# A feed-forward stage with one beside-step per product, low parts split row by row, and residual rows fetched one step sooner

## The chip, the cores and the metric

The kernel runs on one core of a Trainium2 chip. The metric is the time of one execution in device microseconds (us), and the number that counts is the median over runs. The engines are named as the profile names them: PE is TensorE (matmuls), PEld its weight loads, DVE is VectorE, ACT is ScalarE, POOL is GpSimd, SP is SyncE, which here only issues DMAs.

## What is computed

One layer of a streaming encoder, for 2048 prompt tokens and 32 tokens of a running stream, 2080 in all, with 1024 channels: a group of four mixers behind one input projection, and then a gated feed-forward block. The change touches only the second.

```python
x = x + jnp.einsum('ble,ed->bld', mix, w_out[l])
f = rms_norm(x, g_ffn[l])
hid = jax.nn.silu(jnp.einsum('bld,df->blf', f, w_gate[l])) * jnp.einsum('bld,df->blf', f, w_up[l])
x = x + jnp.einsum('blf,fd->bld', hid, w_down[l])
...
y = rms_norm(x, g_final)
```

The hidden width (D_FF) is 2816. All is float32.

## The kernel before

Precision: each float32 operand is split into a high part `hi` (rounded to the PE's fp32r type by an ACT copy) and a low part `lo = x - hi` (a subtraction on POOL or DVE). Each product is three matmuls: w_hi·x_hi, w_lo·x_hi, w_hi·x_lo.

The mixers fill the first 655 us. The feed-forward stage behind them is the other 1470 us. It goes over the tokens in three passes of two chunks each (346 or 348 tokens per chunk), and in each pass over 11 groups `g` of hidden columns. For a group it forms the gate block and then the up block. Each block is a 2x2 block product done with seven products instead of eight; their seven operands, sums and differences of normalized rows, are called p1, p5, p7, p6, p2, p3, p4 in the order of use (`ORDER`). One product is 12 matmuls of 128x128 weights by 346 columns (`wide`, lines 1134 to 1136). After each product about one or two finished pieces of the down projection run (`down`, lines 1149 to 1151), each of six matmuls into one of three PSUM banks, which DVE adds to the residual rows `xs` (line 1152). A "step" is one product with what belongs to it, so a group has 14 steps and a pass 154.

What stands beside the products, on engines whose order is written out by hand:

- **Evacuation of products.** DVE adds a product to a kept sum (lines 1205, 1207, 1227, 1235), multiplies gate and up (1237), ACT makes the high part of the hidden rows (1240) and DVE the low part (1241). In an up block the last four of the seven products have this work, the first three have none.
- **Weights.** DVE forms sums of weight quarters (1050, 1051, 1054, 1057), ACT rounds them (1019), POOL makes their low parts (1020).
- **Beside-work.** Generators in a list `ahead`, of which only the first is advanced in this stage (`active[0] = 1`). `sums_of` makes the next pass's seven operands: per channel row it loads four rows (line 902), waits two turns, then does seven DVE steps (906 to 941) and stores them to `td` in DRAM. `finish` normalizes the rows of the pass that has ended: seven steps of an ACT square and a DVE addition (1347, 1349), then eight DVE scalings (1403), each behind a load issued two rows ahead (1378). After each step of `finish` stands a `yield WAIT`.
- **fill(budget)** is called once per product, after its matmuls have been queued and before its evacuation. It advances the first generator until the budget is used up or the generator says WAIT. A step costs 0.55 to 0.6; the budget is 1.2 (or 0.8) in a gate block and 0.6 (or 0.6) in an up block, and what is overdrawn is owed (`debt`).
- **part(p, name)** turns a stored operand into hi and lo: a load of 128 x 1384 (958), an ACT copy (960) and the subtraction (963), which POOL does for the first two of four rows and DVE for the other two, one instruction each. This happens for 5 operands at the start of the stage, and for 7 in the last up block of the first and of the second pass (a "turn").
- **turn_over**: when the last pieces of a pass are added, its rows are written out (`away`, 1425) and the next pass's residual rows are loaded into the same tile four steps later (`residual`, 1446).

DVE, PE, ACT, POOL and SP each work through their instructions in the order written, so an instruction that waits holds up those behind it.

Of the kernel before, what the change touches and what calls it, by code (L numbers as in the profile page):

```python
# [7 lines left out]
F32 = mybir.dt.float32  # L8
# [26 lines left out]
FPASSES = ((0, 1), (2, 3), (4, 5))  # L35
NG = NFB // 2
H = KT // 2
# [48 lines left out]
def trunk_kernel(ctx: ExitStack, tc: tile.TileContext, a):  # L86
    nc = tc.nc
# [16 lines left out]
    def col(name, i):  # L104
# [5 lines left out]
        out=ident, in_=ident, compare_op=ALU.not_equal, fill=1.0, base=0,  # L110
# [144 lines left out]
    WAIT, LATE, DONE = object(), object(), object()  # L255

    debt = [0.0]

    def fill(budget):
        budget -= debt[0]  # L260
        late = []
        i = 0
        while budget > 0 and i < min(active[0], len(ahead)):
            step = next(ahead[i], DONE)
            if step is DONE:
                ahead.pop(i)
            elif step is WAIT or step is LATE:
                if step is LATE:
                    late.append(ahead[i])
                i += 1  # L270
            else:
                budget -= step
        while budget > 0 and spare:
            step = next(spare[0], DONE)
            if step is DONE:
                spare.pop(0)
            elif step is WAIT:
                break
            else:
                budget -= step  # L280
        for g in late:
            while (step := next(g, DONE)) is not WAIT:
                if step is DONE:
                    ahead.remove(g)
                    break
                budget -= step
        debt[0] = max(-budget, 0.0)
# [3 lines left out]
    def need(*names):  # L291

        for name in names:
            for _ in made[name]:
                pass

    def start(name, gen, spot=None):
        made[name] = gen
        ahead.insert(len(ahead) if spot is None else spot, gen)
# [79 lines left out]
    with ExitStack() as st:  # L379
# [402 lines left out]
        h = {}  # L782
# [164 lines left out]
    def place(p, name):  # L947
        pool, tag, bufs = {"p1": (wgt, "p1", 1), "p5": (wgt, "p5", 1)}.get(name, (bigp, "big", NCH))
        t = pool.tile([P, 2, H * FN], F32R, tag=tag, name="f_" + name, bufs=bufs)
        hi, lo = t[:, 0], t[:, 1]  # L950
        f[p][name] = rows_in(hi, p), rows_in(lo, p)
        return hi, lo

    def part(p, name):

        n = FCH[FPASSES[p][0]]
        hi, lo = place(p, name)
        nc.sync.dma_start(out=lo[:, : H * n].bitcast(F32), in_=td[p, name][:, : H * n])
        yield
        nc.scalar.copy(out=hi[:, : H * n], in_=lo[:, : H * n].bitcast(F32))  # L960
        yield
        for eng, o in ((nc.gpsimd, slice(0, H // 2 * n)), (nc.vector, slice(H // 2 * n, H * n))):
            eng.tensor_sub(out=lo[:, o], in0=lo[:, o].bitcast(F32), in1=hi[:, o].bitcast(F32))  # L963

    def first_operands():

# [174 lines left out]
    step = [0]  # L1141
# [24 lines left out]
    budget = [1.0]  # L1166
    events = []

    def at(k, fn):

        events.append((step[0] + k, fn))
        events.sort(key=lambda e: e[0])


    def block(p, evac, after=lambda k: None):
# [5 lines left out]
        def form(name, b, fresh=True, less=0.0):  # L1181
            if fresh:
                bank[b] = ps_mm.tile([P, 512], F32, tag="mm", name="pw")[:, :n]
            w = wq.take(step[0])
            wide(w, f[p][name], n, bank[b], fresh, True)
            fill(budget[0] - less * (budget[0] > 1))
# [183 lines left out]
    def finish(c):  # L1370

        n = FCH[c]
        got = {}

        def load(k):
            if k < KT:
                got[k] = row("xf")[:, :n]
                nc.sync.dma_start(out=got[k], in_=away[c, k // H][:, k % H * n : (k % H + 1) * n])

        def rows(k):  # L1380
            load(k + 2)
            return got.pop(k)

        load(0)
        load(1)
        yield WAIT
        gen = norm_scales(c, rows)
        while True:
            try:
                v = next(gen)  # L1390
            except StopIteration as e:
                r = e.value
                break
            yield v
            if v == 0.55:
                yield WAIT
        load(0)
        load(1)
        yield WAIT
        y = a["y"][P * KT * FO[c] : P * KT * (FO[c] + n)].rearrange("(p f) -> p f", p=P)  # L1400
        for k in range(KT):
            x = rows(k)
            nc.vector.scalar_tensor_tensor(
                out=x, in0=x, scalar=col("g_final", k), in1=r[:, :n], op0=ALU.mult, op1=ALU.mult
            )
            nc.sync.dma_start(out=y[:, k * n : (k + 1) * n], in_=x)
            yield 0.55
            yield WAIT
# [11 lines left out]
    def turn_over(p, h):  # L1420

        for i, c in enumerate(FPASSES[p]):
            n = FCH[c]
            away[c, h] = dramp.tile([P, H * FN], F32, tag="away_%d_%d" % (c, h), name="away", bufs=1)
            nc.sync.dma_start(out=away[c, h][:, : H * n], in_=halfs[c, h][:, : H * n])
            at(4, lambda i=i: residual(FPASSES[p + 1][i], h))
        if h:
            at(8, lambda: [start(("finish", c), finish(c)) for c in FPASSES[p]])

# [11 lines left out]
    def residual(c, h):  # L1441

        n = FCH[c]
        t = halfs[c, h] = late.tile([P, H * FN], F32, tag="xs", name="xs", bufs=4)
        v = t[:, : H * n].rearrange("p (k n) -> p k n", n=n)
        nc.sync.dma_start(out=v, in_=x2d[:, h * H : (h + 1) * H, FO[c] : FO[c] + n])
        for k in range(H):
            xs[c, h * H + k] = v[:, k]

    last = len(FPASSES) - 1  # L1450
    def put_part(p, name, first=1):

        gen = part(p, name)
        for k in (first, first + 2):
            at(k, lambda: next(gen))
        at(first + 3, lambda: [None for _ in gen])
# [14 lines left out]

    while ("squares", 3) not in made:
        next(made["fstats", 3])
    active[0] = 1
    for p in range(len(FPASSES)):
        for g in range(NG):
            if g == 2 and p < last:
                start(("sums", p + 1), sums_of(p + 1))
            before = after = lambda k: None
            if p == 0 and g == 0:  # L1480
                before = first_parts
            if p < last and g == NG - 1:
                need(("sums", p + 1))
                after = lambda k: put_part(p + 1, ORDER[k])
            gen = None
            if p < last or g < NG - 1:
                gen = quarters(g)
            hid = ffn_pair(p, g, before, after, gen)
            if gen:
                down_later(p, g, hid, gen)  # L1490
# [3 lines left out]
    n = FCH[cb]  # L1494
# [36 lines left out]
    def by_pool(c, k, rs):  # L1531
# [2 lines left out]
        nc.scalar.activation(out=g[:, :n], in_=x, func=AF.Copy, scale=col("g_final", k))  # L1534
        nc.gpsimd.tensor_mul(out=x, in0=g[:, :n], in1=rs[:, :n])

    while ahead:
        fill(100.0)
    for m in range(KT):
# [115 lines left out]
```

## Time and profile before

| what | value |
|---|---|
| median of 3 runs | 2127.08 us (2125.25 to 2128.69) |
| the profiled execution, its own time | 2125.5 us |
| its span | 2123.8 us |
| PE busy | 2027.5 us (95%) |
| DVE busy | 1444.6 us (68%) |
| POOL busy | 1138.5 us (54%) |
| ACT busy | 767.5 us (36%) |
| granted PE clock, mean | 0.982 |

The span is from the first to the last instruction of the program; 1.7 us of the execution's time lie around it. A busy time counts an engine's instructions, not its waits.

### The profile page before, as it was taken

The page shows a single profiled execution, that of the slowest core. Times are in us where ns is not written, and L with a number is a line of the kernel's source. Part 1 is how long each engine was busy: PE and PEld are TensorE (multiplying, and loading weights), DVE is VectorE, ACT ScalarE, POOL GpSimd, SP SyncE. Part 2 cuts the span into 40 slices and gives each one's busy share as a digit, 9 for nine tenths or more (in the row PEclk, how much of TensorE's full clock was granted, in tenths as well). Part 3 has the DMA queues.
Part 4 walks back from the last instruction along what each step waited for, and adds up shares of the span by engine and source line. Part 5 has one row for each costly group of instructions (what it writes and reads, how often), then busy time and mean ns, then how long its engine had stood idle before and what let it go on. Part 6 is the DMA issues. An engine that isn't in the chain of part 4 may idle for free.

```text
span 2123.8 us, 31916 instructions
## 1 busy us (share of the span) xinstructions
PE 2027.5 (95%) x11902; PEld 1980.8 (93%) x11902; DVE 1444.6 (68%) x2207; ACT 767.5 (36%) x1472; POOL 1138.5 (54%) x891
## 2 busy tenths in 40 slices
PE   8699998999997999999999999999999999999997
PEld 7689997899897999999998999999998999999997
DVE  3896599499576677556557676787557577656555
ACT  5423232332334333333334343333334333333332
POOL 2523352243335655656668565666667556655664
PEclk9899998999998999999999999999999999999998
DMA  7634233113367445222224534543224534422221
GB/s 214 177 94 112 71 116 112 41 61 124 108 168 206 137 136 153 85 71 78 78 99 146 188 97 128 159 151 124 75 86 148 195 103 136 133 70 75 75 80 59
DMA packets 152011, 247.88 MB, mean 117 GB/s; under 512 B 23440, under 2 KB 101008, under 8 KB 151216
## 3 DMA queue, kind: packets, MB, share of 16 engines
q1 hardware_dynamic: 149136, 245.67, 37.4%
q8 instruction: 94, 1.54, 0.3%
q14 instruction: 61, 0.50, 0.1%
q10 hardware_dynamic: 2720, 0.18, 0.1%
HBM read 209.42 MB, written 36.36 MB: 116 GB/s over the span
## 4 chain that ended last, share of the span: by engine, by line
PE 51%; DVE 18%; issue 11%; POOL 10%; DMA 7%; ACT 2%; SPq 1%; POOLq 0%; DVEq 0%; ACTq 0%
PE pw L1136 8%; PE pw L1134 8%; PE pw L1135 8%; DVE cv L726 6%; POOL wlo L1020 6%; PE pd L1150 5%; PE pd L1149 5%; PE pd L1151 5%; PE ps L230 4%; PE ps L232 4%; PE ps L231 3%; POOL dlo L1277 2%; DMA line<-rt 2%; DMA xk<-in_x 1%; POOL f_p L963 1%
## 5 line engine op out<-in xcount | busy, mean ns | idle before, releaser
L1136 PE MATMUL pw<-f_p,whi 128*128 128x346 f32 (+1 forms) x1848 | 598.4, 324 | 10.6 <-POOL f_p L963 10.5
L1134 PE MATMUL pw<-f_p,whi 128*128 128x346 f32 (+1 forms) x1848 | 597.5, 323 | 9.0 <-DVE sg L1227 6.0
L1135 PE MATMUL pw<-f_p,wlo 128*128 128x346 f32 (+1 forms) x1848 | 596.3, 323 | 0.0
L1020 POOL TENSOR_TENSOR wlo<-sum,whi 128x512 fp32r<-128x512 f32 x264 | 354.6, 1348 | 288.7 <-ACT whi L1019 285.7
L1152 DVE TENSOR_TENSOR xs<-pd,xs 128x346 f32<-128x346 f32 (+1 forms) x528 | 262.7, 512 | 240.3 <-PE pd L1151 240.2
L1136 PEld LDWEIGHTS pw<-f_p,whi 128*128 128x128 f32 x1848 | 350.1, 189 | 13.6 <-POOL f_p L963 13.6
L1134 PEld LDWEIGHTS pw<-f_p,whi 128*128 128x128 f32 x1848 | 351.5, 190 | 11.7 <-issue 8.3
L1135 PEld LDWEIGHTS pw<-f_p,wlo 128*128 128x128 f32 x1848 | 350.3, 190 | 0.3 <-POOL wlo L1020 0.3
L1277 POOL TENSOR_TENSOR dlo<-raw,dhi 128x256 fp32r<-128x256 f32 x256 | 223.0, 891 | 227.3 <-ACT dhi L1276 224.6
L1149 PE MATMUL pd<-hhi,dhi 128*128 128x346 f32 (+1 forms) x1024 | 330.4, 323 | 15.0 <-DVE xs L1152 15.0
L1150 PE MATMUL pd<-hhi,dlo 128*128 128x346 f32 (+1 forms) x1024 | 329.7, 322 | 0.1
L138 POOL TENSOR_TENSOR wlo<-raw,whi 128x1024 fp32r<-128x1024 f32 x67 | 183.9, 2749 | 269.9 <-ACT whi L137 268.1
L1151 PE MATMUL pd<-hlo,dhi 128*128 128x346 f32 (+1 forms) x1024 | 328.5, 321 | 0.0
L1020 POOL TENSOR_TENSOR wlo<-raw,whi 128x512 fp32r<-128x512 f32 x199 | 275.4, 1392 | 36.6 <-ACT whi L1019 36.4
L1019 ACT CAST whi<-sum 128x512 fp32r<-128x512 f32 x264 | 163.8, 621 | 295.7 <-DVE sum L1054 106.4
L230 PE MATMUL ps<-hi,whi 128*128 128x416 f32 x640 | 236.0, 369 | 8.5 <-ACT hi L214 4.1
L231 PE MATMUL ps<-hi,wlo 128*128 128x416 f32 x640 | 229.5, 359 | 6.6 <-POOL wlo L138 6.0
L232 PE MATMUL ps<-lo,whi 128*128 128x416 f32 x640 | 230.9, 361 | 3.2 <-POOL lo L207 3.0
L726 DVE SCALAR_TENSOR_TENSOR cv<-z,par,cv 128x416 f32<-128x416 f32 (+2 forms) x180 | 216.4, 1263 | 1.0 <-ACT cv L720 0.9
L1149 PEld LDWEIGHTS pd<-hhi,dhi 128*128 128x128 f32 x1024 | 192.8, 188 | 19.8 <-DVE xs L1152 19.2
L1150 PEld LDWEIGHTS pd<-hhi,dlo 128*128 128x128 f32 x1024 | 192.5, 188 | 1.9 <-POOL dlo L1277 1.5
L1151 PEld LDWEIGHTS pd<-hlo,dhi 128*128 128x128 f32 x1024 | 193.0, 189 | 0.0
(185 smaller groups left out, 2863.0 us busy)
## 6 DMA issues: line engine op xcount, KB each, us to landing
raw<-in_w_up SPq DMA_DIRECT2D x132, 256.0 KB
raw<-in_w_gate SPq DMA_DIRECT2D x128, 256.0 KB
raw<-in_w_down SPq DMA_DIRECT2D x256, 128.0 KB
raw<-in_w_in SPq DMA_DIRECT2D x43, 512.0 KB
raw<-in_w_out SPq DMA_DIRECT2D x24, 512.0 KB
f_p<-td SPq DMA_DIRECT2D x14, 692.0 KB
xt<-in_xt SPq DMA_DIRECT2D x20, 416.0 KB
x<-in_x SPq DMA_DIRECT2D x5, 1664.0 KB
```

What stands on the lines that cost most here:

```text
L230: nc.tensor.matmul(out, whi, xhi, start=start and k == 0, stop=False)
L231: nc.tensor.matmul(out, wlo, xhi, start=False, stop=False)
L232: nc.tensor.matmul(out, whi, xlo, start=False, stop=stop and k == n - 1)
L726: nc.vector.scalar_tensor_tensor(out=cv[:, t, :n], in0=z[:, t, j : j + n], scalar=col("w_conf", 31 * t + j), in1=cv[:, t, :n], op0=ALU.mul ...
L1020: nc.gpsimd.tensor_sub(out=lf, in0=src, in1=hf.bitcast(F32))
L1134: nc.tensor.matmul(ps, whi[:, k], xhi[:, k, :n], start=start and k == 0, stop=False, **more)
L1135: nc.tensor.matmul(ps, wlo[:, k], xhi[:, k, :n], start=False, stop=False, **more)
L1136: nc.tensor.matmul(ps, whi[:, k], xlo[:, k, :n], start=False, stop=stop and k == H - 1, **more)
L1149: nc.tensor.matmul(ps, whi, hhi[:, :n], start=i == 0, stop=False)
L1150: nc.tensor.matmul(ps, wlo, hhi[:, :n], start=False, stop=False)
L1151: nc.tensor.matmul(ps, whi, hlo[:, :n], start=False, stop=i == 1)
L1277: nc.gpsimd.tensor_sub(out=lf, in0=raw, in1=hf.bitcast(F32))
```

## The change

Three edits. From the start of the three passes on, `fill` ends after one step that did work, whatever the budget says (the flag `single`). The low parts of an operand are made by four instructions of one row each, the first on POOL and three on DVE. And the residual rows of the next pass are asked for three steps after the others were sent away, where it was four.

```diff
             else:
-                budget -= step
+                budget = 0 if single[0] else budget - step
...
-        for eng, o in ((nc.gpsimd, slice(0, H // 2 * n)), (nc.vector, slice(H // 2 * n, H * n))):
-            eng.tensor_sub(out=lo[:, o], in0=lo[:, o].bitcast(F32), in1=hi[:, o].bitcast(F32))
+        for k in range(H):
+            o = slice(k * n, (k + 1) * n)
+            (nc.vector if k else nc.gpsimd).tensor_sub(
+                out=lo[:, o], in0=lo[:, o].bitcast(F32), in1=hi[:, o].bitcast(F32)
+            )
...
-            at(4, lambda i=i: residual(FPASSES[p + 1][i], h))
+            at(3, lambda i=i: residual(FPASSES[p + 1][i], h))
...
     active[0] = 1
+    single[0] = True
...
+    single[0] = False
     while ahead:
         fill(100.0)
```

What it moves, in three places. The line numbers of the changed kernel are up to seven higher.

First, the instructions of DVE in the second pass's second up block, where `finish` squares a chunk's rows (`ssum<-ssum,sq` is its step). Before:

```order
L1349 TENSOR_TENSOR ssum<-ssum,sq 128x348
L1235 TENSOR_TENSOR u_11229<-pw,u_11335 128x346
L1237 TENSOR_TENSOR sg<-u_11229,sg 128x346
L1241 TENSOR_TENSOR hlo<-sg,hhi 128x346
L1152 TENSOR_TENSOR xs<-pd,xs 128x346
L1054 TENSOR_TENSOR sum<-sum,raw 128x512
L1349 TENSOR_TENSOR ssum<-ssum,sq 128x348
L1235 TENSOR_TENSOR u_11335<-pw,u_11335 128x346
L1237 TENSOR_TENSOR sg<-u_11335,sg 128x346
L1241 TENSOR_TENSOR hlo<-sg,hhi 128x346
L1152 TENSOR_TENSOR xs<-pd,xs 128x346
L1349 TENSOR_TENSOR ssum<-ssum,sq 128x348
```

The same products on DVE in the changed kernel:

```order
L1239 TENSOR_TENSOR u_11253<-pw,u_11359 128x346
L1241 TENSOR_TENSOR sg<-u_11253,sg 128x346
L1245 TENSOR_TENSOR hlo<-sg,hhi 128x346
L1156 TENSOR_TENSOR xs<-pd,xs 128x346
L1058 TENSOR_TENSOR sum<-sum,raw 128x512
L1353 TENSOR_TENSOR ssum<-ssum,sq 128x348
L1239 TENSOR_TENSOR u_11359<-pw,u_11359 128x346
L1241 TENSOR_TENSOR sg<-u_11359,sg 128x346
L1245 TENSOR_TENSOR hlo<-sg,hhi 128x346
L1156 TENSOR_TENSOR xs<-pd,xs 128x346 x2
L1061 TENSOR_TENSOR sum<-raw,sum 128x512
L1353 TENSOR_TENSOR ssum<-ssum,sq 128x348
```

A step of `finish` stood before every product's evacuation; now it stands before every second one, because the WAIT behind it takes a product of its own. `sums_of`, which did up to two or three steps in a product of a gate block, does one.

Second, DVE at the first turn, the low parts of two operands (`f_p`) among the last up block's evacuations. Before:

```order
L1237 TENSOR_TENSOR sg<-pw,sg 128x348
L1241 TENSOR_TENSOR hlo<-sg,hhi 128x348
L1152 TENSOR_TENSOR xs<-pd,xs 128x348
L963 TENSOR_TENSOR f_p_10272<-f_p_10272 128x692
L1235 TENSOR_TENSOR u_10212<-pw,u_10321 128x348
```

And in the changed kernel:

```order
L1241 TENSOR_TENSOR sg<-pw,sg 128x348
L1245 TENSOR_TENSOR hlo<-sg,hhi 128x348
L1156 TENSOR_TENSOR xs<-pd,xs 128x348
L965 TENSOR_TENSOR f_p_10282<-f_p_10282 128x346 x3
L1239 TENSOR_TENSOR u_10222<-pw,u_10331 128x348
```

One instruction of two rows became three of one row in the same place. On POOL each `f_p` row reads 128x346 where it read 128x692, also in the same place.

Third, SP after the first half of a pass's rows has been sent away. Before:

```order
L1425 DMA away<-xs 128x1392 x2
L1265 DMA raw<-in_w_down 128x256 x4
L1446 DMA xs<-x2d 128x4x346 x2
L1027 DMA raw<-in_w_up 128x512 x2
```

And in the changed kernel:

```order
L1429 DMA away<-xs 128x1392 x2
L1450 DMA xs<-x2d 128x4x346 x2
L1269 DMA raw<-in_w_down 128x256 x4
L1031 DMA raw<-in_w_up 128x512 x2
```

The residual rows now stand ahead of four loads of down weights. PE's own order is the same up to the place of four small matmuls per chunk of `finish`, and nothing changes ahead of the feed-forward stage.

## Rows read from the trace of the kernel before

**Rows 1.** The page's first line.
```profile
span 2123.8 us, 31916 instructions
```
**Rows 2.** Windows: us, busy PE PEld DVE ACT POOL (instructions), clock, DMA, GB/s.
```profile
655.00:700.00 45.00, 33.98 (x180) 31.78 (x178) 23.62 (x31) 15.43 (x25) 27.89 (x19) 0.81 0.76 211
...
1120.00:1160.00 40.00, 34.92 (x207) 32.49 (x206) 33.73 (x42) 19.15 (x33) 33.73 (x23) 1.00 0.38 130
```
**Rows 3.** Waits of PE, 655 to 700: who, for whom, total us, times, longest.
```profile
PE pw L1136 <- POOL f_p L963: 5.5, 2, 3.2
PE pw L1134 <- ACT f_p L960: 3.0, 1, 3.0
PE tok L147 <- DVE ssum L346: 2.5, 1, 2.5
```
**Rows 4.** Waits of PE, 700 to 1120.
```profile
PE pw L1134 <- DVE sg L1227: 3.4, 2, 3.1
```
**Rows 5.** Waits of PE, 1120 to 1160, the first turn.
```profile
PE pd L1149 <- DVE xs L1152: 2.5, 3, 1.2
PE pw L1136 <- POOL f_p L963: 2.5, 3, 1.4
```
**Rows 6.** Waits of PE, 1160 to 1600.
```profile
PE pd L1149 <- DVE xs L1152: 5.0, 3, 2.4
PE pw L1134 <- DVE sg L1227: 1.7, 3, 1.0
```
**Rows 7.** Waits of PE, 1640 to 2060, the row that differs from rows 6.
```profile
PE pw L1134 <- DVE sg L1227: 1.0, 2, 0.8
```
**Rows 8.** Waits of DVE, 700 to 2060, three of eleven rows.
```profile
DVE ssum L1349 <- ACT sq L1347: 20.9, 17, 3.8
DVE xf L906 <- DMA xf<-x2d: 11.6, 5, 4.1
...
DVE xf L1403 <- DMA xf<-away: 7.9, 4, 3.6
```
**Rows 9.** Timeline of DVE, 1218 to 1236: start, us, instruction, [idle before <- releaser].
```profile
1223.82 1.31 DVE L1349 TENSOR_TENSOR ssum<-ssum,sq 128x348 f32<-128x348 f32 x1 [1.14 <-ACT sq L1347]
...
1226.66 0.52 DVE L1241 TENSOR_TENSOR hlo<-sg,hhi 128x346 fp32r<-128x346 f32 x1 [0.55 <-ACT hhi L1240]
```
**Rows 10.** Timeline of PE, 1228 to 1236, its two waits.
```profile
1227.66 0.42 PE L1149 MATMUL pd<-hhi,dhi 128*128 128x346 f32 x1 [0.91 <-DVE xs L1152]
...
1233.41 0.43 PE L1149 MATMUL pd<-hhi,dhi 128*128 128x346 f32 x1 [1.68 <-DVE xs L1152]
```
**Rows 11.** Timeline of DVE, 1120 to 1158, the first turn.
```profile
1131.76 1.39 DVE L1241 TENSOR_TENSOR hlo<-sg,hhi 128x348 fp32r<-128x348 f32 x1 [0.55 <-ACT hhi L1240]
...
1133.50 0.86 DVE L963 TENSOR_TENSOR f_p<-f_p 128x692 fp32r<-128x692 f32 x1
...
1137.83 1.93 DVE L963 TENSOR_TENSOR f_p<-f_p 128x692 fp32r<-128x692 f32 x1
```
**Rows 12.** Timeline of POOL, the same stretch.
```profile
1130.79 1.98 POOL L963 TENSOR_TENSOR f_p<-f_p 128x692 fp32r<-128x692 f32 x1
1135.75 1.34 POOL L1020 TENSOR_TENSOR wlo<-sum,whi 128x512 fp32r<-128x512 f32 x1 [2.98 <-ACT whi L1019]
1137.06 1.95 POOL L963 TENSOR_TENSOR f_p<-f_p 128x692 fp32r<-128x692 f32 x1
```
**Rows 13.** Groups by form, DVE, 700 to 2060: busy us, mean ns, idle before.
```profile
L963 DVE TENSOR_TENSOR f_p<-f_p 128x692 fp32r<-128x692 f32 x14 | 20.8, 1488 | 0.0
```
**Rows 14.** Groups by form, POOL, 640 to 2060.
```profile
L963 POOL TENSOR_TENSOR f_p<-f_p 128x692 fp32r<-128x692 f32 x14 | 28.7, 2048 | 0.0
```
**Rows 15.** Timeline of SP's DMA issues, 1164 to 1176.
```profile
1164.26 1.49 SPq L1425 DMA_DIRECT2D away<-xs  x2
1165.80 5.94 SPq L1265 DMA_DIRECT2D raw<-in_w_down  x4
1171.84 2.06 SPq L1446 DMA_DIRECT2D xs<-x2d  x2
```

More of the change, by code (lines that the diff above doesn't have):

```diff
@@ L257, in trunk_kernel @@
     debt = [0.0]
+    single = [False]
     def fill(budget):
```

## The prediction

> **What bounds the kernel now.** I read the page first. Its span is 2123.8 us [rows 1]; the profiled execution took 2125.5, so 1.7 lie around the span, and the median of the three runs shown, 2127.1, is 1.6 above that execution. PE is busy 95% of the span, so the feed-forward stage is bound by PE's own matmuls, which the change leaves as they are. What a change of order can win there is the time in which PE stands still. So the second view was the list of PE's waits, cut into stretches so that each cause has its place.
>
> Between 700 and 2060 us four stretches are quiet or almost so, and their waits have one look: PE waits for DVE, either to free a PSUM bank (the piece of the down projection at line 1149 waits for the addition into `xs`) or to finish with a product (line 1134 waits for `sg`). That is 3.4 us in the first pass [rows 4], 5.0 + 1.7 in the second [rows 6], and 5.0 + 1.0 in the third, whose `xs` row reads like the one of the second [rows 6, 7]. Together 16.1 us. The two turns, each of 40 us, have 2.5 + 2.5 us [rows 5], with the same two sums in the turn from 1600 to 1640, half of it for POOL's low parts of the next operands: 10.0 us for both. The start of the stage has 11.0 us: 5.5 for POOL's low parts, 3.0 for a copy whose load landed late, 2.5 for DVE's sums of squares [rows 3], and its granted clock is 0.81, a mix of the two levels [rows 2]. So about 37 us of the span are in reach of this change, and no more.
>
> **One beside-step per product.** DVE is far from busy over a pass, so why does PE wait for it? The timeline of DVE shows it: a step of `finish` adds a square that ACT has only just been asked for, so DVE stands 1.14 us in front of it, and then takes 1.31 for the addition [rows 9]. That is 2.45 us in one product, and the evacuation of that product and the next one queue behind it. Over 700 to 2060 us DVE lost 20.9 us in this way, 11.6 for the loads of `sums_of` and 7.9 for those of the scalings [rows 8]. Four such steps in the last four products of one up block are 4 x 2.45 = 9.8 us of delay, and PE lost 0.91 + 1.68 = 2.6 of them [rows 10]; the other 7.2 were taken up by the PSUM banks and by DVE's free time. The change leaves two such steps in these four products (order, first place): 4.9 us, under the 7.2 that were taken up without a wait of PE. For `finish` the waits should therefore go; also because each load has twice as many products to land in before its scaling.
>
> For `sums_of` the up blocks keep their one step per product; the gate blocks lose their second one. Its load is no longer asked for in the product whose last step SP must see stored first, but in the next one, so the 4.1 us for which DVE stood [rows 8], behind which PE waited 3.1 [rows 4], should shrink to a fraction. But the work is the same and takes more products, so some blocks that were free of it now carry it. I take three quarters of 16.1: **-12.5 us**. The ends: all of it, -16, and a quarter, -4, if the delay is spread and not shortened. The list of steps must also end in time: the sums of the third pass now end just ahead of the last group, with three steps in one product instead of one. That is two steps of about 1 us more on DVE, in a product whose delay can be as long as the other 7.2 were: nothing, at most +2.
>
> **Low parts by rows.** This happens 5 times at the start and 7 times at each turn. POOL's instruction of two rows takes 2.05 us [rows 14]; of one row, 1.0. On DVE two rows take 0.86 alone, as at 1133.50 between two instructions of POOL, and 1.93 while POOL subtracts too, as at 1137.83 [rows 11, 12]; the mean is 1.49 [rows 13]. One row is 0.52 alone, the price of the hidden rows' low part, which has the same shape [rows 9]. So three rows cost 3 x 0.52 = 1.56 alone and at most 1.5 x 1.93 = 2.9 beside a busy POOL; against 1.49 that is +0.1 to +1.4 us per operand on DVE, which is busy 33.7 of 40 us at a turn [rows 2]. Against this stands what the other DVE instructions get back when POOL is busy a microsecond less: the low part of the hidden rows took 1.39 beside POOL against 0.52 alone [rows 9, 11], so 0.87 each time. I take +0.3 us per operand after both, 2 us per turn on DVE, of which PE feels half, since DVE has a pause here and there: +1.0. POOL's queue at the turn gets 1.0 us shorter per operand, and the three waits for it are at most 1.4 long [rows 5], with four or more operands ahead of each: all 2.5 should go. So -1.5 per turn, **-3 us** for both. The ends: -5 per turn if `xs` waits go as well, and 7 x 1.4 = 9.8 on DVE, of which two thirds reach PE, less 2.5, so +4 per turn.
>
> The Trainium skill speaks against this edit: its page "VectorE: DVE Perf Modes", section "Rules for kernel authors", asks for fewer VectorE instructions, since each pays its own drain. The trace agrees as far as three rows at 0.52 against two at 0.86 go [rows 9, 11]. By that rule alone the 19 operands would cost VectorE 19 x 0.70 = 13 us; if all of it reached PE, the sum below would end near 2124.
>
> At the start the same edit lengthens DVE's way to the sums of squares (two operands come right before them, +0.5 us each) and shortens POOL's two waits of 5.5 by 1.0 each. In between stands the wait for a load, 3.0, whose issue on SP hangs on that same DVE work, so the delay is not absorbed there. **-0.5 us**, with ends of -4 and +3, since the clock there is not at its full level all the time and may be granted earlier or later.
>
> **Rows at step three.** SP had issued the residual loads 7.6 us after the rows were sent away, behind four loads of down weights that held it 5.9 us [rows 15]. One step sooner they stand ahead of these loads. No row of DVE's waits has line 1152 waiting for a DMA [rows 8], so nothing is won. The price: SP may now stand until the rows have left the tile, but two of the four weight loads were not issued before the last microsecond of their 5.9 anyway. **0 us**, at most +2.
>
> **Sum.** -12.5 - 3 - 0.5 = -16. From 2125.5 that is 2109.5, and with the 1.6 by which the median lies higher, 2111.
>
> **The rivals.**
>
> 1. The delay is spread, not shortened. A step still holds DVE for its 2.45 us, and there are now twice as many blocks with `finish` in them; `sums_of` keeps its rhythm in the up blocks. For it: a step's own length does not change [rows 9]. Against it: the waits come in runs of steps [rows 10], and the runs are cut. Then -4 - 1 = -5: 2122.
> 2. More than that: DVE gets ahead everywhere and both kinds of waits at the turns go too, -16 - 10 - 3 = -29: 2098. For it: at a turn the `xs` waits follow instructions that stretched beside POOL [rows 11]. Against it: the three rows.
> 3. Slower: the rows on DVE become the limit of the turns. If three rows take 2.9 us each time, the turns cost +4 each and the start +3; with rival 1's -4 in the passes the sum is +7: 2134. It decides from a mean of about 0.9 us per row on. For it: DVE is busy 33.7 of 40 us there [rows 2]. Against it: POOL's half is what stretches DVE, and it is halved. The Trainium skill's "GPSIMD Engine Reference", section "Key points", says that GpSimd shares its SBUF interfaces with VectorE instructions of two SBUF inputs, which is how I read the 0.86 and 1.93; so less POOL work should help.
> 4. Edit three costs what it can, or the late sums do, with the forecast gain halved: -8 + 4 = -4, 2123, no difference that can be told.
>
> **How the numbers follow.** What a measurement of this kernel can tell from no change is about 0.2%, 4.3 us, so from 2122.8 to 2131.3 counts as the same. Forecast (gain of 8 to 24 us) 0.62, rival 1 with gains of 3 to 8 us 0.15, rival 2 0.11, rival 3 0.07, rival 4 0.05. Faster: 0.62 + 0.11 and two thirds of rival 1, 0.10, is 0.83; same: a third of rival 1, rival 4 and a small part of rival 3, 0.11; slower: 0.06. The forecast's own range is 2103 to 2119. For 8 in 10, half of rival 2 below and most of rival 1 above are taken in: 2100 to 2123.
>
> **What would show it.** Right: PE's waits for `xs` and `sg` between 700 and 2060, outside the turns, fall from 16.1 to about 4 us; its waits for POOL's `f_p` at the turns from 5.0 to near 0; DVE's `f_p` rows have a mean of 0.55 to 0.75 us; DVE's waits for ACT's squares do not shrink much in sum, but no longer stand in neighbouring products. Wrong: new waits of PE for `xs` in up blocks that had none, or turns with more than 5 us of waits each. The prediction fails most easily in the share of the 16.1 us that really goes, and in DVE's load at the turns.

## The result, and the profile after

The changed kernel takes 2113.8 us (median of 5 runs, 2110.8 to 2118.0) against 2127.1 us (5 runs, 2125.3 to 2128.7): a ratio of 0.9945, 95% interval 0.9931 to 0.9958. It is faster by 13.3 us where 16 were forecast. The profiled execution took 2113.76 us. One execution among all the experiments, of 2453.9 us at a granted clock of 0.75, is left out of the times below. Line numbers in the rows shown are up to four higher than before.

The page's first line of the changed kernel. The span fell by 11.8 us against [rows 1].

```profile
span 2112.0 us, 31921 instructions
```

The windows of the changed kernel: the first pass, the first turn, the second pass (columns as in [rows 2]).

```profile
700.00:1115.00 415.00, 414.84 (x2601) 414.07 (x2600) 263.57 (x446) 153.64 (x320) 256.61 (x218) 1.00 0.33 102
1115.00:1155.00 40.00, 31.57 (x174) 30.22 (x173) 36.59 (x53) 17.96 (x29) 26.22 (x22) 0.91 0.36 121
1155.00:1595.00 440.00, 439.52 (x2768) 438.61 (x2767) 300.97 (x502) 166.89 (x352) 272.84 (x232) 1.00 0.42 132
```

Two opposite things stand in this table. In the passes PE is now busy 414.84 of 415 and 439.52 of 440 us: it hardly stands still at all. In the turn it is busy 31.57 of 40 us, where [rows 2] had 34.92, DVE is busy 36.59 (33.73), and the granted clock, which was 1.00, is 0.91, a mix of the two levels. So the change won in the passes and lost in the turns. PE's waits say behind whom. First the two rows of the passes (700 to 1115, then 1155 to 1595), behind them the two of the first turn (1115 to 1155):

```profile
PE pw L1138 <- DVE sg L1231: 0.2, 1, 0.2
...
PE pw L1138 <- DVE sg L1231: 0.5, 1, 0.5
...
PE pd L1153 <- DVE xs L1156: 4.9, 3, 2.4
PE pw L1138 <- DVE sg L1231: 3.4, 1, 3.4
```

In the third pass there is no row at all. The 16.1 us of [rows 4, 6, 7] have become 0.7. At the first turn the 2.5 us behind POOL [rows 5] are gone, but the waits behind DVE are 8.3 instead of 2.5; the second turn reads 5.1 and 3.3. At the start:

```profile
PE pw L1140 <- POOL f_p L965: 3.7, 2, 2.7
PE tok L147 <- DVE ssum L347: 3.4, 1, 3.4
PE pw L1138 <- ACT f_p L961: 2.9, 1, 2.9
```

POOL's part fell by 1.8 us and DVE's rose by 0.9, against [rows 3].

A wait can cost more than its length, because the matmuls behind it can come slower for a moment: in the kernel before, PE waits 3.1 us in the first pass, until 804.9, and from 804 to 810 the granted clock is 0.72, a mix of the two levels. So I also worked out, from PE's timeline, how far apart neighbouring matmuls start beyond 0.16 us, counted where they are over 0.25 us apart, and summed this "loss" by place:

| loss of PE, us | before | after | difference |
|---|---|---|---|
| start (640 to 720) | 17.5 | 17.0 | -0.5 |
| two turns | 7.3 + 7.3 | 12.3 + 11.0 | +8.7 |
| the three passes outside the turns | 5.4 + 10.3 + 8.0 | 0.3 + 1.7 + 1.0 | -20.6 |
| sum | 55.8 | 43.3 | -12.5 |

The sum answers to the 11.8 us of the span.

The groups by form of the changed kernel, 700 to 2050, give the cause at the turns (columns as in [rows 13]):

```profile
L965 DVE TENSOR_TENSOR f_p<-f_p 128x346 fp32r<-128x346 f32 x42 | 39.9, 1002 | 0.0
L965 POOL TENSOR_TENSOR f_p<-f_p 128x346 fp32r<-128x346 f32 x14 | 16.9, 1205 | 0.0
```

One row takes DVE 1.00 us in the mean, not 0.52. Neighbouring instructions overlap by 0.08 us in the profile; with that counted once, the three rows of an operand keep DVE busy for 39.9 / 14 = 2.85 us. It was 1.49 for two rows in one instruction [rows 13].

### The profile page after: what moved, and what is told of

Read it like the earlier page. It is cut to its first block, busy times and chain, and to the rows that moved or that the text cites. A ratio compares the mean times of both kernels' runs of the same rounds, so it can differ in the third digit from the quotient of the medians.

```text
span 2112.0 us, 31921 instructions
## 1 busy us (share of the span) xinstructions
PE 2028.9 (96%) x11902; PEld 1989.9 (94%) x11902; DVE 1451.7 (69%) x2245; ACT 767.8 (36%) x1472; POOL 1125.0 (53%) x891
## 4 chain that ended last, share of the span: by engine, by line
PE 67%; DVE 16%; DMA 6%; issue 6%; POOL 4%; ACT 1%; SPq 0%; DVEq 0%; POOLq 0%; ACTq 0%
PE pw L1140 12%; PE pw L1138 12%; PE pw L1139 12%; PE pd L1154 7%; PE pd L1155 7%; PE pd L1153 7%; DVE cv L727 5%; PE ps L232 3%; PE ps L230 3%; PE ps L231 3%; POOL wlo L1024 2%; DVE f_p L965 2%; DMA xk<-in_x 1%; DMA line<-rt 1%; DMA raw<-in_w_in 1%
## 5 line engine op out<-in xcount | busy, mean ns | idle before, releaser
L1138 PE MATMUL pw<-f_p,whi 128*128 128x346 f32 (+1 forms) x1848 | 597.7, 323 | 10.3 <-DVE sg L1231 7.4
L1153 PEld LDWEIGHTS pd<-hhi,dhi 128*128 128x128 f32 x1024 | 193.4, 189 | 13.3 <-DVE xs L1156 12.2
```

The costliest lines, as they stand in the source:

```text
L1138: nc.tensor.matmul(ps, whi[:, k], xhi[:, k, :n], start=start and k == 0, stop=False, **more)
L1153: nc.tensor.matmul(ps, whi, hhi[:, :n], start=i == 0, stop=False)
```

## The experiments

Each kernel was timed beside the kernel before on its own chip, where the latter took 2121.0 to 2122.5 us; the ratios are against that, and a gain given in us is the ratio's.

Two theories of the rows stood against each other. **Share** (B where the expectations on rows use letters): DVE got three rows of four, and rows beside POOL stretch in proportion, so the way to help is to give DVE fewer rows. **Count** (C, in the last two D): each DVE instruction has to wait for a whole POOL instruction, so the price is per instruction, and the way to help is to give the same rows in fewer instructions. In the first two expectations, A is the theory on record and B what the trace of the changed kernel suggested.

### The three parts, each alone

One beside-step per product, on the kernel before:

```diff
+    single = [False]
...
-                budget -= step
+                budget = 0 if single[0] else budget - step
...
+    single[0] = True
...
+    single[0] = False
```

> The kernel before with one beside-step per product and nothing else. The theory on record (A: steps -12.5, rows -3): 2127 - 12.5 = about 2114.5, slower than the whole change by the 3 that the rows were to bring. The theory from the changed kernel's trace (B: the steps bring nearly all of the 16.1 us of waits and some restart time, the rows cost): about 2127 - 18 = 2109, faster than the whole change. Under both, PE's waits outside the turns are at or below 4 us, under B below 1; the turns keep the 5.0 us of waits each that they had before, half of it for POOL.

Measured: 2098.7 us, ratio 0.9893 [0.9875, 0.9910], or -22.7 us. PE's waits of this kernel from 1155 to 1575 and at the first turn:

```profile
PE pw L1135 <- DVE sg L1228: 0.2, 1, 0.2
...
PE pd L1150 <- DVE xs L1153: 2.5, 3, 1.2
PE pw L1137 <- POOL f_p L964: 2.5, 3, 1.4
```

This part clears the passes by itself, and leaves the first turn as it was [rows 5]. It is faster alone than in the whole change.

Low parts row by row, on the kernel before:

```diff
-        for eng, o in ((nc.gpsimd, slice(0, H // 2 * n)), (nc.vector, slice(H // 2 * n, H * n))):
-            eng.tensor_sub(out=lo[:, o], in0=lo[:, o].bitcast(F32), in1=hi[:, o].bitcast(F32))
+        for k in range(H):
+            o = slice(k * n, (k + 1) * n)
+            (nc.vector if k else nc.gpsimd).tensor_sub(
+                out=lo[:, o], in0=lo[:, o].bitcast(F32), in1=hi[:, o].bitcast(F32)
+            )
```

> The kernel before with the low parts row by row, one on POOL and three on DVE, and nothing else. A: 2127 - 3 = 2124, the turns at 3.5 us of waits of PE each, DVE rows below 0.75 us. B: the three rows take about 3.1 us per operand as in the changed kernel (1.05 a row), the turns wait 8.4 us each instead of 5.0, so about 2127 + 6 = 2133; waits of 16 us outside the turns as before.

Measured: 2133.1 us, 1.0056 [1.0042, 1.0069], or +11.9 us: this part alone makes the kernel slower. PE's waits at its first turn, 1112 to 1155:

```profile
PE pd L1152 <- DVE xs L1155: 5.4, 4, 2.4
PE pw L1137 <- DVE sg L1230: 4.1, 1, 4.1
```

The loss as defined above is 12.4 and 13.5 us at its turns, 11.2 more than before; the start gains 0.5. That accounts for the time.

Residual rows at step three, on the kernel before:

```diff
-            at(4, lambda i=i: residual(FPASSES[p + 1][i], h))
+            at(3, lambda i=i: residual(FPASSES[p + 1][i], h))
```

> The kernel before with the residual rows asked for at step three and nothing else. Both theories: 2127, no difference that can be told, every wait of PE within 0.5 us of what it was. A rival: the rows' earlier return shortens the turns; then the waits for xs at the turns fall below 2.5 us each and the time is 2124 or less.

Measured: 2121.6 us, 0.9997 [0.9988, 1.0007]; the waits at the turn read as in [rows 5]. Nothing, as forecast. The three parts add up: -1.07% + 0.56% - 0.03% = -0.54%, and the whole change measured -0.55%.

### Which steps pay

The limit of one step for `sums_of` alone, and for `finish` alone, each on the kernel before with the flag of the first experiment and only this condition changed:

```diff
-                budget = 0 if single[0] else budget - step
+                budget = 0 if single[0] and ahead[i].gi_code.co_name == "sums_of" else budget - step
```

> The kernel before with one beside-step per product for the sums of the next pass alone; the normalization of the last pass keeps its step before every product, rows and step of the residual rows as before. If the gain of the steps alone (ratio 0.989) lies in the normalization, where a step was followed by a product of its own: PE's waits of 5 to 6 us in the second and in the third pass stay, the 3.4 of the first pass and the 0.5 near 1456 us go, -5 us, ratio 0.998. If it lies in the sums: ratio near 0.992.

Measured: 2111.5 us, 0.9958 [0.9941, 0.9975], -8.9 us.

```diff
-                budget = 0 if single[0] else budget - step
+                budget = 0 if single[0] and ahead[i].gi_code.co_name == "finish" else budget - step
```

> The same for the normalization of the last pass alone; the sums keep two steps in a product of a gate block. If the gain lies in the normalization: its waits in the second and third pass go, the 3.4 of the first pass stay, -15 to -18 us, ratio 0.992. If it lies in the sums: ratio 0.997 or above. With the run before, the two should add up to the 0.989 of both.

Measured: 2105.6 us, 0.9930 [0.9915, 0.9945], -14.9 us. PE's waits of the one in its second pass (1149 to 1584), and of the other in its first pass (700 to 1105):

```profile
PE pd L1150 <- DVE xs L1153: 5.0, 3, 2.4
PE pw L1135 <- DVE sg L1228: 1.0, 1, 1.0
```

```profile
PE pw L1135 <- DVE sg L1228: 3.4, 2, 3.0
```

With `sums_of` paced, the 3.4 us of the first pass go, while 6.0 stay in the second and 5.1 in the third, nearly all for `xs`. With `finish` paced the 3.4 stay, 3.1 are left in the second pass (2.1 of them for `sg`) and none in the third. So the first pass's waits belong to `sums_of`, and most of the other two's to `finish`. The two gains, 0.42% and 0.70%, add up to the 1.07% of both within their intervals.

### Fewer rows for DVE

From here on each kernel is the changed kernel with another split of the low parts. Two rows on each engine, still one instruction per row:

```diff
-            (nc.vector if k else nc.gpsimd).tensor_sub(
+            (nc.vector if k > 1 else nc.gpsimd).tensor_sub(
```

> The changed kernel, but of the four one-row instructions the first two on POOL and the last two on DVE: the share of before, cut into rows. If DVE's share is what costs at the turns (B), DVE takes about 2 us per operand instead of 3.1, the turns wait 4 to 5 us each, less of it for POOL since its first row is ready sooner, and the time is about 2107. If the number of instructions is what costs, the turns stay at 8 us each and the time near 2113.

Measured: 2100.5 us, 0.9895 [0.9879, 0.9912]. The same kernel ran again for its trace.

> The changed kernel with two of four rows on POOL and two on DVE, once more, since the profile of its first run came from an execution at a clock of 0.75 and its waits can't be read. Theory B (DVE's share at the turns is what the rows cost): waits of PE at the turns 4 to 5 us each, rows on DVE about 1.0 us each because POOL is busy all the time, time level with the kernel that has the steps alone (ratio about 0.989). Rival C (the number of instructions costs): turns above 7 us each; its first timing, 0.9895, already speaks against C.

Measured: 2101.2 us, 0.9900 [0.9883, 0.9916]. By form, 700 to 2050, and PE's waits at its first turn:

```profile
L965 POOL TENSOR_TENSOR f_p<-f_p 128x346 fp32r<-128x346 f32 x28 | 33.4, 1215 | 0.0
L965 DVE TENSOR_TENSOR f_p<-f_p 128x346 fp32r<-128x346 f32 x28 | 26.4, 983 | 0.0
```

```profile
PE pd L1153 <- DVE xs L1156: 3.7, 3, 1.9
PE pw L1138 <- DVE sg L1231: 0.6, 1, 0.6
```

Better than three rows by half a per cent, and nothing waits for POOL. But this does not tell the theories apart: fewer rows are also fewer instructions. The price of a row stayed at 0.98 us, though DVE does a third fewer of them.

Three rows on POOL, one on DVE:

```diff
-            (nc.vector if k else nc.gpsimd).tensor_sub(
+            (nc.vector if k > 2 else nc.gpsimd).tensor_sub(
```

> The changed kernel with three of four rows on POOL and one on DVE. B alone: DVE pays 1 us per operand, waits for xs and sg at the turns fall below 2 us each. But POOL's queue gets 1 us longer per operand, and PE already waited 2.5 us per turn for POOL's second row when POOL had two: waits for POOL of 4 to 8 us per turn. Sum: no better than two and two, ratio 0.989 to 0.993. If the ratio falls below 0.988, POOL's queue has room and the split of before was not the best.

Measured: 2106.9 us, 0.9927 [0.9910, 0.9944]. PE's waits at its first turn:

```profile
PE pw L1140 <- POOL f_p L965: 3.1, 7, 0.6
PE pd L1154 <- POOL dlo L1281: 0.9, 1, 0.9
```

Now POOL is the limit; one row on DVE still takes 0.95 us.

All four rows on DVE, one instruction each:

```diff
-            (nc.vector if k else nc.gpsimd).tensor_sub(
+            nc.vector.tensor_sub(
```

> The changed kernel with all four rows on DVE, none on POOL. What was assumed for the prediction (POOL's own half of the low parts is what stretches DVE's): without it the rows take about 0.55 us each, 2.2 per operand, less than the 3.1 of the changed kernel, and the turns wait less than its 8.4 us. B (POOL's weights stretch them as well, so DVE pays per row whoever else runs): rows still near 0.9 us, 3.6 per operand, the turns above 8.4 us each, ratio 0.996 to 1.0.

Measured: 2106.9 us, 0.9927 [0.9911, 0.9943]. More rows on DVE than in the change, in more instructions, and yet it is no slower (the intervals overlap). Its groups by form (700 to 2050), and two operands in DVE's timeline (start, us, instruction), with POOL's beside them:

```profile
L965 DVE TENSOR_TENSOR f_p<-f_p 128x346 fp32r<-128x346 f32 x56 | 38.1, 738 | 0.0
```

```profile
1135.90 1.79 DVE L965 TENSOR_TENSOR f_p<-f_p 128x346 fp32r<-128x346 f32 x4
1138.05 4.64 DVE L965 TENSOR_TENSOR f_p<-f_p 128x346 fp32r<-128x346 f32 x4
```

```profile
1136.28 2.56 POOL L1024 TENSOR_TENSOR wlo<-sum,whi 128x512 fp32r<-128x512 f32 x1 [3.85 <-ACT whi L1023]
1138.80 3.09 POOL L1024 TENSOR_TENSOR wlo<-raw,whi 128x512 fp32r<-128x512 f32 x2
```

The sizes expected for this run, 0.55 or 0.9 us per row, were both off, and these rows show why: one operand's four rows take 1.79 us, as four rows alone would, and the next one's take 4.64 beside POOL's low parts of weights (`wlo`, 1138.80 to 1141.89). The mean of 0.74 is a mix of the two. POOL has no `f_p` rows here at all, and DVE is still held up beside it; so it is not only POOL's own quarter of the operand that DVE waits for, but POOL's subtractions for the weights as well. And the price can fall on POOL: beside the four quick rows its `wlo` is recorded with 2.56 us, where the 442 of this kernel from 700 to 2050 have a median of 1.30. The second turn shows the same pair (four rows in 1.79, `wlo` 2.57). Which of the two engines gives way was not tried.

### The same rows in fewer instructions

One row on POOL and three on DVE, as in the change, but DVE's three in one instruction:

```diff
-        for k in range(H):
-            o = slice(k * n, (k + 1) * n)
-            (nc.vector if k else nc.gpsimd).tensor_sub(
-                out=lo[:, o], in0=lo[:, o].bitcast(F32), in1=hi[:, o].bitcast(F32)
-            )
+        for eng, o in ((nc.gpsimd, slice(0, n)), (nc.vector, slice(n, H * n))):
+            eng.tensor_sub(out=lo[:, o], in0=lo[:, o].bitcast(F32), in1=hi[:, o].bitcast(F32))
```

> The changed kernel with the same share, one row on POOL and three on DVE, but the three rows in one instruction of 128x1038. B: DVE's instruction takes about 3 us beside POOL, as the three did, PE's waits at the turns stay near 8 us each, perhaps plus a few tenths because the first row is released later, ratio about 0.994 to 0.996. C: two of three fixed costs fall away, the turns fall towards 5 us, ratio about 0.990.

Measured: 2094.7 us, 0.9867 [0.9852, 0.9882], the lowest of all: 28 us below the kernel before. By form, 700 to 2050, and PE's waits at its first turn (1104 to 1149):

```profile
L964 DVE TENSOR_TENSOR f_p<-f_p 128x1038 fp32r<-128x1038 f32 x14 | 21.4, 1527 | 0.0
L964 POOL TENSOR_TENSOR f_p<-f_p 128x346 fp32r<-128x346 f32 x14 | 19.6, 1400 | 0.0
```

```profile
PE pd L1150 <- DVE xs L1153: 1.6, 2, 1.2
PE pw L1137 <- POOL f_p L964: 1.0, 1, 1.0
```

The share is that of the change; the price of an operand on DVE is about half, 1.53 us against 2.85, and the turn loses 2.6 us of waits instead of 8.3. Share is refuted, count stands.

Two instructions on DVE for the same three rows:

```diff
-        for k in range(H):
-            o = slice(k * n, (k + 1) * n)
-            (nc.vector if k else nc.gpsimd).tensor_sub(
-                out=lo[:, o], in0=lo[:, o].bitcast(F32), in1=hi[:, o].bitcast(F32)
-            )
+        for eng, o in (
+            (nc.gpsimd, slice(0, n)), (nc.vector, slice(n, 2 * n)), (nc.vector, slice(2 * n, H * n))
+        ):
+            eng.tensor_sub(out=lo[:, o], in0=lo[:, o].bitcast(F32), in1=hi[:, o].bitcast(F32))
```

> The changed kernel with one row on POOL and three on DVE, the three in two instructions, of one row and of two. D: two waits for POOL per operand on DVE instead of three (changed kernel, 8.4 us of idle PE per turn) or one (one-and-three, 2.7): idle PE of 4.5 to 6.5 us per turn, DVE about 2.2 us per operand, ratio 0.990 to 0.992. If the price goes by columns: as the changed kernel or the one-and-three kernel, no middle.

Measured: 2100.9 us, 0.9904 [0.9889, 0.9919]. By form:

```profile
L966 DVE TENSOR_TENSOR f_p<-f_p 128x692 fp32r<-128x692 f32 x14 | 23.5, 1678 | 0.0
...
L966 DVE TENSOR_TENSOR f_p<-f_p 128x346 fp32r<-128x346 f32 x14 | 10.0, 715 | 0.0
```

And all four rows in one DVE instruction, none on POOL:

```diff
-        for k in range(H):
-            o = slice(k * n, (k + 1) * n)
-            (nc.vector if k else nc.gpsimd).tensor_sub(
-                out=lo[:, o], in0=lo[:, o].bitcast(F32), in1=hi[:, o].bitcast(F32)
-            )
+        o = slice(0, H * n)
+        nc.vector.tensor_sub(out=lo[:, o], in0=lo[:, o].bitcast(F32), in1=hi[:, o].bitcast(F32))
```

> The changed kernel with all four rows of an operand's low part in one instruction on DVE, none on POOL. Theory D (each DVE instruction of two SBUF inputs waits once for the POOL instruction that is running, and POOL's for DVE's; the price goes by the number of instructions, not by columns): about 1.5 us alone and 1.5 to 2.2 beside POOL, against 2.2 to 3 for four instructions; turns at or below the 2.7 us of idle PE of the one-and-three kernel unless the wait for the first row costs more; ratio 0.986 to 0.989. By the amount that DVE takes over (theory B): the turns as with four instructions, 7.5 us each, ratio 0.993.

Measured: 2096.8 us, 0.9884 [0.9870, 0.9899]. By form, and PE's waits at its first turn:

```profile
L964 DVE TENSOR_TENSOR f_p<-f_p 128x1384 fp32r<-128x1384 f32 x14 | 25.9, 1850 | 0.0
```

```profile
PE pw L1135 <- DVE sg L1228: 2.3, 1, 2.3
PE pd L1150 <- DVE xs L1153: 1.5, 2, 1.1
```

The runs side by side; DVE's busy time is per operand at the turns, with overlaps counted once:

| rows on DVE | instructions | DVE, us | PE's waits, first turn, us | ratio |
|---|---|---|---|---|
| 3 | 3 (the change) | 2.85 | 8.3 | 0.9945 |
| 3 | 2 | 2.32 | 5.8 | 0.9904 |
| 3 | 1 | 1.53 | 2.6 | 0.9867 |
| 4 | 4 | 2.72 | 7.4 | 0.9927 |
| 4 | 1 | 1.85 | 4.0 | 0.9884 |
| 2 | 2 | 1.89 | 4.3 | 0.9900 |
| 2 | 1 (first experiment) | 1.49 | 5.0, half of it for POOL | 0.9893 |

Within three rows, each instruction less takes 0.5 to 0.8 us off an operand; within four, three less take 0.9 off. The three kernels with the lowest ratios, 0.9867, 0.9884 and 0.9893, have overlapping intervals.

## Why the prediction was right in its sum and wrong in two terms

The time fell in the range, near the forecast, because two errors cancelled: the steps gave more than the term said, and the rows took where the term said they would give. That the sum came so near is luck.

**One beside-step per product: the waits went as forecast, the size was too small and the picture behind it only partly right.** The term was -12.5 us; the trace shows -20.6, and alone it measured -22.7. Two things were off in the size. I took three quarters of the 16.1 us, and all but 0.7 went. And I counted only PE's waits, not the slower matmuls behind each: the 16.1 us of waits stand in 23.6 us of loss before, about 1.5 us per us of wait. With that factor the waits that each half removed come near its time: of 16.1 us, pacing `sums_of` left 11.1 and so removed 5.0, 7.4 with the factor, against 8.9 us measured; pacing `finish` left 6.5 and removed 9.6, 14.1 against 14.9.

The sum that let the waits of `finish` go was misread. Four steps stand one behind the other in the stretch of [rows 9]:

```profile
1218.29 1.31 DVE L1349 TENSOR_TENSOR ssum<-ssum,sq 128x348 f32<-128x348 f32 x1
...
1228.19 0.66 DVE L1349 TENSOR_TENSOR ssum<-ssum,sq 128x348 f32<-128x348 f32 x1 [0.58 <-ACT sq L1347]
...
1231.62 1.30 DVE L1349 TENSOR_TENSOR ssum<-ssum,sq 128x348 f32<-128x348 f32 x1 [1.08 <-ACT sq L1347]
```

With the one at 1223.82 they hold DVE for 1.31, 2.45, 1.24 and 2.38 us, 7.4 together and not 4 x 2.45 = 9.8. What was taken up without a wait of PE was then 4.8, not 7.2, and two steps of 2.45 are not below it. That the waits of `finish` went all the same did not follow from this sum.

What I said of DVE was half right. DVE's waits of the changed kernel, 700 to 2050:

```profile
DVE ssum L1353 <- ACT sq L1351: 17.4, 16, 1.5
DVE xf L1407 <- DMA xf<-away: 13.0, 4, 5.0
DVE xf L907 <- DMA xf<-x2d: 8.4, 2, 4.4
```

The waits for squares did not shrink much (20.9 in [rows 8]), as forecast. But the step that let the loads' waits shrink to a fraction is wrong: the longest wait for a load of `sums_of` is 4.4 us, where it was 4.1 (in sum they fell from 11.6 to 8.4), and the scalings lost 13.0 us, where they lost 7.9, although each load had twice as many products to land in. Together the three rows fell only from 40.4 to 38.8. So DVE's waits are hardly shorter. Rival 1's picture, spread and not shortened, fits best; its conclusion, that little would be won, was wrong. In the changed kernel DVE's waits of 4.0 to 5.0 us for a load are followed by waits of PE of at most 0.5; before, those of 3.5 to 4.1 were followed by 0.3, 0.8, 1.0 and 3.1. That a free product behind each step takes the delay up is the likely reason, and not a shown one: the waits also stand at other places of their blocks than before, and no run moved them without the pacing.

**Low parts by rows: wrong sign.** The term was -3; the trace shows +8.7, and alone it measured +11.9. The waits for POOL at the turns went, all 2.5 us of each turn, as forecast, though one row takes POOL 1.21 us and not 1.0. Two steps failed. The first is "I take +0.3 us per operand after both, 2 us per turn on DVE". The same instructions at the first turn, from the first operand's rows on, in the kernel before and in the one with the rows alone (columns as in [rows 2]):

```profile
1121.50:1161.92 40.42, 35.34 (x210) 32.91 (x209) 33.65 (x41) 18.85 (x32) 34.74 (x24) 1.00 0.37 125
```

```profile
1117.20:1161.29 44.09, 34.49 (x199) 32.87 (x199) 37.73 (x55) 19.01 (x32) 29.21 (x25) 0.96 0.34 115
```

DVE's busy time grew by 4.1 us (3.8 at the second turn), twice the 2 that were taken. Added up instruction by instruction, the rows went from 10.4 to 21.0 us, 1.5 more per operand, and the other 33 instructions gave back 5.6, which is 0.8 per operand. So the giving back was seen rightly, and the price of the rows was not: the bound of 2.9 for three contended rows, scaled by columns, was taken for the extreme, and the mean was 2.85. The second step that failed is "of which PE feels half": PE's waits behind DVE grew at the first turn by 5.8 us in the changed kernel and by 7.0 with the rows alone, more than DVE's own busy time did. The prediction's own sign of being wrong, turns with more than 5 us of waits each, is there with 8.3 and 8.4. The reading of the rows failed before that. Beside POOL, two rows took 1.93 against 0.86 alone, 1.07 more; the low part of the hidden rows, one row, took 1.39 against 0.52, 0.87 more [rows 9, 11]. The surcharge was nearly the same for half the columns: that points to a price per instruction, and the rows of before already held it. DVE's timeline of the changed kernel at the first turn, and POOL's in the same place:

```profile
1128.50 1.37 DVE L965 TENSOR_TENSOR f_p<-f_p 128x346 fp32r<-128x346 f32 x3
...
1143.26 0.51 DVE L1156 TENSOR_TENSOR xs<-pd,xs 128x348 f32<-128x348 f32 x1
1143.68 3.83 DVE L965 TENSOR_TENSOR f_p<-f_p 128x346 fp32r<-128x346 f32 x3
```

```profile
1131.26 1.33 POOL L1024 TENSOR_TENSOR wlo<-sum,whi 128x512 fp32r<-128x512 f32 x1 [5.54 <-ACT whi L1023]
...
1142.92 1.56 POOL L1024 TENSOR_TENSOR wlo<-raw,whi 128x512 fp32r<-128x512 f32 x1
1144.44 1.21 POOL L965 TENSOR_TENSOR f_p<-f_p 128x346 fp32r<-128x346 f32 x1
1145.61 1.53 POOL L1024 TENSOR_TENSOR wlo<-raw,whi 128x512 fp32r<-128x512 f32 x1
```

At 1128.50 POOL has nothing to do, and three rows take 1.37 us. At 1143.68 POOL has three instructions one behind the other, and the three rows take 3.83. Taken singly they end at 1144.86, 1146.03 and 1147.52, each about 0.4 us, the time of a row alone, behind the end of one POOL instruction (1144.48, 1145.65, 1147.14). Here the two engines take turns, whole instruction by whole instruction, and DVE pays once per instruction. It is not always one by one: in the run with all rows on DVE, rows went on at 0.51 us each while one instruction of POOL is recorded as running. At 1143.26 the addition into `xs`, one of whose inputs comes from PSUM, keeps its 0.51 us beside POOL's instruction of 1142.92. The products' evacuation queues behind those 3.83 us, and PE waits 3.4 us for `sg` at 1149.

The Trainium skill's page "SBUF — State Buffer", section "Who interferes with whom", says of a VectorE instruction with two SBUF inputs that it contends with a GpSimd instruction that reads SBUF, and of the port pair which they share that it is an exclusive lock. The trace agrees: three rows in 3.83 us against 1.37. The rule of the Trainium skill that the prediction weighed, to keep the number of VectorE instructions low, was the right warning; what the runs show of the price is the wait for POOL (1.37 us for three rows without it, 3.83 beside it).

Rival 3 was right about the turns and their price: from a mean of 0.9 us per row on it gave +4 per turn, and at 1.00 the trace shows +5.0 and +3.7. What spoke against it, that POOL's half is what stretches DVE, was refuted by the run with no rows on POOL, where four rows still took 4.64 us beside `wlo`. As a whole it did not come true, because the passes gave 20.6 us.

**Start: -0.5, measured -0.5** in the loss, and again -0.5 with the rows alone. The two opposite shifts are there, 1.8 us less for POOL and 0.9 more for DVE. But three kernels whose start is that of before (steps alone, `sums_of` paced, rows at step three) show -1.1, -1.8 and -1.8 there, so a term of this size can't be told from how the start varies.

**Rows at step three: 0, measured 0.** SP's queue in the changed kernel:

```profile
1163.00 3.20 SPq L1429 DMA_DIRECT2D away<-xs  x2
1166.29 3.70 SPq L1450 DMA_DIRECT2D xs<-x2d  x2
1170.04 2.15 SPq L1269 DMA_DIRECT2D raw<-in_w_down  x4
```

SP does stand 3.7 us at the residual rows, and the four weight loads behind them are out at 1172.2, against 1171.7 [rows 15].

**Not settled.** The change with three rows in three instructions lost 8.7 us more at the turns than before, the rows alone 11.2; the waits are almost equal (16.7 and 17.8 us). The rest goes with the granted clock of the turns: where it is 1.00 (before), the loss is 2.3 us more than the waits; at 0.95 and 0.96 it is 2.6 and 2.9 more (the change's second turn, the first with the rows alone), at 0.91 and 0.89 it is 4.0 and 5.2 more (the two others). Why the clock fell at one of these turns longer than at the other was not tried. Whether the kernel with one row on POOL and three in one instruction owes its lead over the steps alone (0.9867 against 0.9893, whose intervals overlap) to POOL's earlier row was not tried apart from the longer DVE instruction.

## What to carry to other kernels

Work that stands in an in-order queue beside a product can be placed so that a step with a wait is followed by a product free of it: here PE's waits outside the turns fell from 16.1 to 0.7 us, though DVE's own waits hardly shrank. Where two engines hold each other up whole instruction by whole instruction, count instructions and not columns: give the engine on which the critical one waits few long instructions. And compare a contended row with its free twin at two sizes before scaling it: a surcharge that does not grow with the size is paid per instruction.

## What the runs showed of the hardware that was not expected

DVE's subtraction of 346 columns took about 0.45 us in a row of them when it was not held up (four in 1.79); beside two instructions of POOL, one behind the other, four took 4.64, of which the three that POOL held up had 1.17 to 1.61 each. Of 1038 columns in one instruction it took 1.53 in the mean. In that kernel POOL pays more: its one row takes 1.40 us, where it takes 1.21 beside three short instructions. Each engine can thus be held up by the other.

PE's granted clock fell from 1.00 to 0.91 over the 40 us of the first turn when its longest waits there had grown to 2.4 and 3.4 us; in the kernel with 2.6 us of waits at that turn it stayed at 1.00 from 1104 to 1149, and the loss was 1.7 us more than the waits, where it was 4.0 more in the changed kernel.
